# One layer of a hybrid decoder trunk: the last tiles' routing and the first experts' preparation in another order

## The chip, the cores and the metric

The kernel runs on 1 core of a Trainium2 chip. TensorE (PE) multiplies, VectorE (DVE) and ScalarE (ACT) work elementwise, GpSimd (POOL) does some elementwise work and issues the indirect transfers, and SyncE (SP) issues most of the other transfers. All of them run side by side and each takes its instructions strictly in the order in which the program emits them. The metric is device microseconds for one execution, the median of several runs.

## What is computed

One layer of a trunk over 1024 tokens of width 1024. A mixer (a causal convolution branch and an mLSTM branch) ends in `x1 = x + gate1 * (merged W_out)`. Its second half is a mixture of experts, which is what the change is about:

```python
h = modulate(rmsnorm(x1, g_norm2), sh2, sc2)
p_grp = softmax(h @ w_rg + b_rg); g_sel = argmax(p_grp)           # one group of 4
le_sel = (h @ w_re + b_re).reshape(T, 4, 8)[t, g_sel[t]]          # its 8 experts
top_p, top_e = top_k(softmax(le_sel), 2)                          # two of them
w_tok = p_grp[g_sel] * top_p / sum(top_p)
y = sum over the two: w_tok * ((silu(h @ w_e_gate[e]) * (h @ w_e_up[e])) @ w_e_down[e])
out = rmsnorm(x1 + gate2 * y, g_final)
```

There are 32 experts; `w_e_gate`, `w_e_up` and `w_e_down` hold 6 MB of each in float32, together about 201 MB.

## The kernel before

**Order.** The schedule is written out by hand: the order in which the Python code calls the engines is the order on each engine. Float32 products are made in three passes of a split pair (`split`: ACT casts the high part, DVE subtracts it to get the low part), so each operand that is split costs one ACT and one DVE instruction.

**Tiles and routing.** Tokens are cut into 8 tiles `t` of 128. For each tile, `products` multiplies the merged branches by `W_out` in 8 steps `k` (halves `hf` of 512 columns; three matmuls a step and half), `residual` adds `x` on DVE, `second_norm` scales and stores `h2` to `h2_d` in DRAM, `router_T` transposes the tile on PE with a copy on ACT, and `router` makes 36 logits. `choose(a, b)` picks group and experts for tiles a to b-1 on DVE, a chain of some 18 small instructions; `weigh(a, b)` makes the weights in three steps (subtractions and three Exp on ACT; reciprocals and products; a split into bfloat16 columns of `Vc`). Both are generators: `fill` runs one step of what the list `lat` holds, `drain` runs all of it. For t = 4 and 5 they are put into `lat`; for tiles 5, 6 and 7 `choose` is called outright.

**Ranks, keys, selections.** `ranks_early` counts, by matmuls over one-hot rows, how many tokens before each one chose the same expert. `set_key` turns this into a slot number for the experts 0 and 1 (`FIX = 2`), which are handled first without knowing how full the others are. `sel_into(r, sl)` compares an iota with the key to get a selection matrix; `first_slots` multiplies it with the token numbers, `index` turns the sums into indices, and `gather` fetches the expert's rows of `h2_d` by an indirect transfer on POOL into `xgs[r]`, which ACT has cleared before. `order_of_experts` (three steps, `places_`) sorts the experts by their counts, gives the list `elist` from which SP takes the weights' addresses, and gives each token its place `pos` in its expert's block. `st_sel(b)` makes the selection of block `b` (two instructions on DVE, one of them 128x2048), `st_slots(b)` its token indices (16 small matmuls on PE, two instructions on DVE) and the gather, `st_x(b)` the transposed and split input, `st_gu` the gate (`wi = 0`) and up (`wi = 1`) products, `st_act` Silu and the product, `st_h` its transposition, `st_down` the down products and the scatter to `y_d`.

**Weights.** The object `W` streams the experts' weights: each load is 1 MB into one of six buffers `big`; SP issues the next load when a buffer has been split or, for pieces marked plain, has been multiplied. Split parts go to five pairs of buffers. `W.split()` forces the next split; `W.take()` hands out a piece, splits up to `nsplit` pieces ahead and issues loads. Gate of expert 0 has four pieces; the first three are split during tiles 1 to 3.

**Blocks.** `units = [[0], [1], [16], [2, 24], [17], [3], ...]`: in unit i of the loop at the end, the products of unit i+1 are woven with the activation and down products of unit i. Blocks 16 to 23 hold two experts with few tokens, 64 rows each; their pieces are all plain, and their matmuls use half of the array's columns.

Of the kernel before, what the change touches and what calls it, by code (L numbers as in the profile page):

```python
# [8 lines left out]
F32 = mybir.dt.float32  # L9
# [33 lines left out]
def hybrid_layer_kernel(ctx: ExitStack, tc: tile.TileContext, x, c, w_ada, b_ada, g_norm1, w_in, b_if,  # L43
# [11 lines left out]
    def tt(o, a, b, op, eng=V):  # L55
        return eng.tensor_tensor(out=o, in0=a, in1=b, op=op)  # L56

    def ts(o, a, s1, op0, s2=None, op1=None, eng=V):
        if op1 is None:
            return eng.tensor_scalar(out=o, in0=a, scalar1=s1, scalar2=None, op0=op0)  # L60
        return eng.tensor_scalar(out=o, in0=a, scalar1=s1, scalar2=s2, op0=op0, op1=op1)
# [1058 lines left out]
    def k3(ap):  # L1120
        return ap.rearrange("p (k q) -> p k q", q=P)
# [85 lines left out]
    lsg = rp.tile([P, NT, NE], F32, name="lsg")  # L1207
    rev = rp.tile([P, EPG], F32, name="rev")
    t4 = [rp.tile([P, NT, NG], F32, name=f"t4{i}") for i in range(3)]
    t8 = [rp.tile([P, NT, EPG], F32, name=f"t8{i}") for i in range(6)]  # L1210
# [125 lines left out]
    def order_of_experts():  # L1336
# [16 lines left out]
        ts(bs[0:NE], idn, rc, OP.mult)  # L1353
        ts(tw[0:NE], ion[0:NE], rc, OP.is_equal)
        yield 0
        psx = mps.tile([P, 512], F32, tag="m", name="psord")
# [10 lines left out]
        yield 0  # L1367
        kp = mo.tile([P, NT, NE], F32, tag="tHL", bufs=2, name="kp")
        ts(kp, rank, float(P), OP.is_ge, float(P * (TWB - FIX - 1)), OP.mult)
        tt(kp, kp, rank, OP.add)  # L1370
        tt(kp, kp, cb(bs, NE), OP.add)
# [104 lines left out]
    for t in range(NT):  # L1476
# [18 lines left out]
        if t < NT - 1:  # L1495
            for k in range(KT):
                products(k, (0, 1))
                if k == 2 and t > 0:
                    router_T(t - 1)
                if k == 5 and t > 0:  # L1500
                    router(t - 1)
                    if t == NT - 2:
                        for _ in choose(t - 1, t):
                            pass
            if t == 0:
                router_const()
            if t in (4, 5):
                a_, b_ = ((0, 3), (3, 5))[t - 4]
                lat.extend((choose(a_, b_), weigh(a_, b_)))
            for _ in range(6 if t < 6 else 20):  # L1510
                fill(0)
            for hf in range(2):
                residual(t, hf)
            second_norm(t)
        else:
            for k in range(KT):
                products(k, (0,))
                if k == 3:
                    router_T(t - 1)
            router(t - 1)  # L1520
            for _ in choose(t - 1, t):
                pass
            residual(t, 0)
            scale_half(t, 0)
            po[t][1] = zps.tile([P, 2, 512], F32, tag="z", name=f"o{t}_1")[:, 0, :]
            for k in range(KT):
                if k == KT - 1:
                    router(t, (0,))
                products(k, (1,))
                if k == 3:  # L1530
                    router_T(t, (0,))
                if k == 5:
                    ranks_early()
                    set_key(slice(0, LT), psr[0][:, 0:LT])
                    S.copy(rank[:, 0:LT], psr[0][:, 0:LT])
    sel01 = uo.tile([P, FIX, NT, P], BF16, tag="ar", bufs=2, name="sel01")
    psf = {}
# [10 lines left out]

    sel_into(0, slice(0, LT))
    yp.release()  # L1550
# [18 lines left out]
    xgs = [e4(f"xg{i}") for i in range(3)]  # L1569
    for g_ in xgs:  # L1570
        S.activation(k3(g_), iota.unsqueeze(1).broadcast_to([P, KT, P]), AF.Copy, scale=0.0)
    for _ in choose(LT, NT):
        pass
# [46 lines left out]
    def ovf_slots(pool, bv, name):  # L1620
# [12 lines left out]
        return idx, wsl, ps, osel  # L1633

    identb = rp.tile([P, P], BF16, name="identb")
    V.tensor_copy(identb, ident)

# [154 lines left out]
    for r in range(FIX):  # L1792
        if r:
            sel_into(r, slice(0, LT))
        sel_into(r, slice(LT, NT))
        first_slots(r, LT if r == 0 else 0, NT)
        idx = mo.tile([P, 1], I32, tag="fidx", name=f"fidx{r}")
        index(mo, idx, psf[r], 0, f"f{r}")
        gather(xgs[r], idx)
        R[r] = dict(xg=xgs[r])  # L1800
# [5 lines left out]
    rest = weigh(LT - 2, NT)  # L1806
    next(rest)
    next(places_)
    st_x(0)
    W.split()  # L1810
    W.split()
    next(rest)
    next(places_)
    for _ in rest:
        pass
    W.nsplit = 4
    st_gu(0, 0, 0, 4)
    for b in blocks_of(2):
        st_sel(b)
    W.split()  # L1820
    W.split()
    st_x(1)
    st_gu(0, 1, 0, 2)
    for b in blocks_of(2):
        st_slots(b)
    st_sel(0)
    st_gu(0, 1, 2, 4)
    st_slots(0, False)
# [36 lines left out]
    for i, unit in enumerate(units):  # L1865
# [3 lines left out]
        st_act(unit[-1])  # L1869
        for b in blocks_of(i + 3) if i else []:  # L1870
            st_slots(b)
# [9 lines left out]
        for b in now:  # L1881
            st_x(b)
        for b in blocks_of(i + 4) if i else []:
            st_sel(b)
        if i == 0:
            for b in units[3]:
                st_sel(b)
        fill(0)
        fill(0)
        if not nxt:  # L1890
# [180 lines left out]
```

## Time and profile before

| what | value |
|---|---|
| median of 3 runs | 1435.85 us (1435.72 to 1435.99) |
| the profiled execution | 1434.2 us, span 1432.4 us from first to last instruction |
| mean granted TensorE clock | 0.963 of full speed |
| busy: PE, DVE, ACT, POOL | 1303.9, 999.9, 513.7, 326.8 us |
| moved by DMA | 337.13 MB |
| last tile's routing to first expert | about 779 to 812 us of the span |

The times in all views count from the start of the span. In a row of the timeline the columns are start, duration, engine, line, operation, what it writes and reads, partitions and elements, and how many are merged; brackets give the idle time of the engine before it and what ended that. Names are those of the program without numbers: `mg` is the tile `x1`, `o` the products with `W_out`, `sel` any selection, `sl` and `slf` slot sums, `tpx` and `tph` transposes of an expert's input and hidden values, `gu` gate and up products, `py` down products, `wh` and `wl` the split weights. A line is often a helper's (L56 `tt`, L60 and L61 `ts`, L64 `stt`, L67 `mm`, L148 the cast in `split`).

### The profile page before, as it was taken

The numbers are of one execution on the slowest core, as the hardware profiler recorded it, in microseconds if no ns is written. First come the engines' busy times: TensorE is split into PE (matmuls) and PEld (weight loads), VectorE is DVE, ScalarE is ACT, GpSimd is POOL, SyncE is SP. The second block draws the span as 40 slices with busy tenths as digits, with TensorE's granted clock in tenths as the row PEclk, the third lists the DMA queues.
The fourth block names the chain that finished last, engine by engine and source line by source line (L and its number), as shares of the span: only waits on it lengthen the run. The fifth ranks groups of instructions, "written<-read, shape, count | busy, mean of one in ns | idle before, by whom it ended". The sixth has DMA issues, their size and how long they took to land. (4 is left out here: it accounts for less than half of the span.)

```text
span 1432.4 us, 17703 instructions
## 1 busy us (share of the span) xinstructions
PE 1303.9 (91%) x6627; PEld 973.3 (68%) x6627; DVE 999.9 (70%) x1371; ACT 513.7 (36%) x682; POOL 326.8 (23%) x265
## 2 busy tenths in 40 slices
PE   4799989999989999999999679999899999999976
PEld 3687888879878888777887445656465565654554
DVE  6979998889976761655556685457676675754587
ACT  5233143333532224411222323335344353533442
POOL 3333455231331310115222010001111111110033
PEclk9799989999999999999999899999999999999998
DMA  9433443333353433444521578899999999999982
GB/s 288 126 118 133 140 140 119 132 118 88 115 175 125 154 114 129 168 155 154 175 102 59 191 259 331 331 379 407 418 414 404 407 401 402 405 385 399 397 337 119
DMA packets 121161, 337.13 MB, mean 235 GB/s; under 512 B 12481, under 2 KB 74221, under 8 KB 96240
## 3 DMA queue, kind: packets, MB, share of 16 engines
q1 hardware_dynamic: 106064, 290.81, 54.4%
q0 software_dynamic: 14528, 43.56, 8.1%
q10 hardware_dynamic: 480, 1.59, 0.3%
q8 instruction: 53, 0.87, 0.2%
q14 instruction: 36, 0.29, 0.1%
HBM read 303.37 MB, written 41.45 MB: 241 GB/s over the span
## 5 line engine op out<-in xcount | busy, mean ns | idle before, releaser
L56 DVE TENSOR_TENSOR wl<-big,wh 128x1024 fp32r<-128x1024 f32 x184 | 224.7, 1256 | 104.5 <-ACT wh L148 103.4
L148 ACT CAST wh<-big 128x1024 fp32r<-128x1024 f32 x184 | 185.5, 1048 | 174.8 <-DMA big<-in_w_e_gate_dram 90.8
L64 DVE SCALAR_TENSOR_TENSOR cacc<-u,vec,cacc 128x1024 f32<-128x1024 f32 x120 | 212.0, 1767 | 2.9
L67 PE MATMUL z<-hH,wh 128*128 128x512 f32 x512 | 166.3, 407 | 7.4 <-DVE hH L377 5.1
L67 PE MATMUL gu<-wh,tHLx 128*128 128x512 f32 x528 | 169.3, 401 | 2.6 <-ACT wh L148 2.6
L67 PE MATMUL z<-hL,wh 128*128 128x512 f32 x512 | 163.0, 400 | 1.4 <-DVE hL L56 1.2
L67 PE MATMUL z<-hH,wl 128*128 128x512 f32 x512 | 162.2, 398 | 0.0
L67 PE MATMUL gu<-big,tFx 128*64 128x512 f32 (+1 forms) x528 | 131.8, 628 | 0.0
L67 PEld LDWEIGHTS gu<-wh,tHLx 128*128 128x128 f32 x528 | 96.7, 189 | 29.5 <-ACT wh L148 9.5
L67 PEld LDWEIGHTS z<-hH,wh 128*128 128x128 f32 x512 | 96.2, 192 | 29.3 <-ACT hH L380 5.1
L67 PEld LDWEIGHTS z<-hL,wh 128*128 128x128 f32 x512 | 97.3, 190 | 26.1 <-DVE hL L56 1.9
L67 PEld LDWEIGHTS z<-hH,wl 128*128 128x128 f32 x512 | 97.3, 190 | 23.6 <-DVE wl L56 0.2
L67 PE MATMUL gu<-wl,tHLx 128*128 128x512 f32 x264 | 106.1, 402 | 7.7 <-DVE wl L56 7.6
L1617 POOL DMA_INDIRECT y_d<-ye,idx x23 | 32.6, 1416 | 339.1 <-DVE ye L64 319.0
L56 DVE TENSOR_TENSOR wl<-raw,wh 128x1024 fp32r<-128x1024 f32 (+1 forms) x45 | 70.7, 1575 | 39.5 <-ACT wh L148 39.5
L67 PEld LDWEIGHTS gu<-big,tFx 128*64 128x64 f32 (+1 forms) x528 | 39.8, 146 | 73.7 <-issue 71.6
L56 POOL TENSOR_TENSOR acc<-acc,ar 128x1024 f32<-128x1024 f32 x24 | 70.5, 2939 | 61.5 <-ACT ar L572 51.8
L67 PE MATMUL zt<-wl,hH 128*128 128x256 f32 (+1 forms) x256 | 76.1, 297 | 4.5 <-DVE wl L56 4.5
L67 PE MATMUL zt<-wh,hH 128*128 128x256 f32 (+1 forms) x256 | 77.3, 302 | 0.8 <-ACT qk L659 0.7
L67 PE MATMUL zt<-wh,hL 128*128 128x256 f32 (+1 forms) x256 | 76.2, 298 | 0.0
L67 PE MATMUL o<-woH,mHL 128*128 128x512 f32 x256 | 72.9, 401 | 0.0
L67 PE MATMUL py<-wh,tHLh 128*128 128x512 f32 x256 | 72.5, 405 | 0.1
(403 smaller groups left out, 2193.2 us busy)
## 6 DMA issues: line engine op xcount, KB each, us to landing
big<-in_w_e_gate_dram SPq DMA_DIRECT2D x64, 1024.0 KB
big<-in_w_e_up_dram SPq DMA_DIRECT2D x64, 1024.0 KB
big<-in_w_e_down_dram SPq DMA_DIRECT2D x64, 1024.0 KB
raw<-in_w_in_dram SPq DMA_DIRECT2D x38, 512.0 KB
ar<-in_w_ada_dram SPq DMA_DIRECT2D x16, 1024.0 KB
araw<-in_w_ada_dram SPq DMA_DIRECT2D x8, 1024.0 KB
y_d<-zero SPq DMA_DIRECT2D x16, 512.0 KB
big<-y_d SPq DMA_DIRECT2D x9, 512.0 KB
```

The costliest lines, as they stand in the source:

```text
L56: return eng.tensor_tensor(out=o, in0=a, in1=b, op=op)
L64: return V.scalar_tensor_tensor(out=o, in0=a, scalar=s, in1=b, op0=op0, op1=op1)
L67: return PE.matmul(o, l, r, start=start, stop=stop)
L148: S.copy(h, src)
L1617: G.indirect_dma_start(out=y_d[:, :], out_offset=bass.IndirectOffsetOnAxis(ap=idx[:, 1:2], axis=0), in_=src, in_offset=None, bounds_check= ...
```

## The change

It reorders what is emitted; nothing is computed differently. Part by part: (1) `identb`, a bfloat16 identity, is made at the set-up. (2) In tile 6, `drain` runs what is left of `weigh(3, 5)` at step k = 1 instead of after the products. (3) In tile 7, `router_T(6)` and `router(6)` come earlier among the first half's products, and in the second half `router_T(7)`, the ranks and the first half of `router(7)` come later. (4) Both selections of tiles 0 to 6 for the experts 0 and 1 are made together before `residual(7, 1)`. (5) The third buffer for gathered rows is cleared later. (6) In `order_of_experts` the first two instructions on `kp` move from the third step to the first. (7) After the three Exp of tiles 5 to 7, ACT runs a Silu on one column. (8) Gate piece 3 of expert 0 is split right behind that, gate pieces 0 to 2 of expert 1 only after the gate products of expert 0 (before: pieces 0 ahead of them, 1 and 2 behind). (9) The selection of block 16 comes before, that of block 0 in front of the up products of expert 0, and both sets of slots behind all of them. (10) In unit 1 of the loop, `st_slots(17)` comes after the gate products of block 16, the transposes of unit 1 and `st_x(2)`. (11) The two `fill(0)` of every unit are gone; the one thing left in `lat`, the check for overflowing experts (`overflow`), runs in unit 4 instead of unit 0.

```diff
+    identb = rp.tile([P, P], BF16, name="identb")
+    V.tensor_copy(identb, ident)
...
+        kp = mo.tile([P, NT, NE], F32, tag="tHL", bufs=2, name="kp")
+        ts(kp, rank, float(P), OP.is_ge, float(P * (TWB - FIX - 1)), OP.mult)
+        tt(kp, kp, rank, OP.add)
         yield 0
...
-        kp = mo.tile([P, NT, NE], F32, tag="tHL", bufs=2, name="kp")
-        ts(kp, rank, float(P), OP.is_ge, float(P * (TWB - FIX - 1)), OP.mult)
-        tt(kp, kp, rank, OP.add)
...
                 products(k, (0, 1))
+                if k == 1 and t == NT - 2:
+                    drain()
...
-            for _ in range(6 if t < 6 else 20):
+            for _ in range(6):
                 fill(0)
...
                 products(k, (0,))
-                if k == 3:
+                if k == 2:
                     router_T(t - 1)
-            router(t - 1)
+                if k == 5:
+                    router(t - 1)
...
             for k in range(KT):
-                if k == KT - 1:
-                    router(t, (0,))
                 products(k, (1,))
-                if k == 3:
+                if k == 4:
                     router_T(t, (0,))
-                if k == 5:
+                if k == 6:
                     ranks_early()
...
+            router(t, (0,))
...
-    sel_into(0, slice(0, LT))
+    for r in range(FIX):
+        sel_into(r, slice(0, LT))
...
-    for g_ in xgs:
+    def clear_xg(g_):
         S.activation(k3(g_), iota.unsqueeze(1).broadcast_to([P, KT, P]), AF.Copy, scale=0.0)
+    for g_ in xgs[0:2]:
+        clear_xg(g_)
...
     for r in range(FIX):
-        if r:
-            sel_into(r, slice(0, LT))
         sel_into(r, slice(LT, NT))
...
     next(places_)
     rest = weigh(LT - 2, NT)
     next(rest)
+    S.activation(mo.tile([P, 1], F32, tag="silu", bufs=1, name="silu"), pio, AF.Silu)
+    W.split()
+    clear_xg(xgs[2])
     next(places_)
     st_x(0)
-    W.split()
-    W.split()
+    next(places_)
     next(rest)
-    next(places_)
     for _ in rest:
         pass
     W.nsplit = 4
-    st_gu(0, 0, 0, 4)
     for b in blocks_of(2):
         st_sel(b)
+    st_gu(0, 0, 0, 4)
+    W.split()
     W.split()
     W.split()
     st_x(1)
-    st_gu(0, 1, 0, 2)
+    st_sel(0)
+    st_gu(0, 1, 0, 4)
     for b in blocks_of(2):
         st_slots(b)
-    st_sel(0)
-    st_gu(0, 1, 2, 4)
     st_slots(0, False)
...
-        for b in blocks_of(i + 3) if i else []:
+        for b in blocks_of(i + 3) if i > 1 else []:
             st_slots(b)
...
         for b in now:
             st_x(b)
+        for b in blocks_of(i + 3) if i == 1 else []:
+            st_slots(b)
...
-        fill(0)
-        fill(0)
+        if i == 4:
+            drain()
```

## Rows read from the trace of the kernel before

**Rows 1.** Windows: length, busy time of PE, PEld, DVE, ACT, POOL; granted clock, DMA share, GB/s.

```profile
803.00:868.00 65.00, 50.44 (x276) 30.95 (x277) 45.94 (x113) 18.64 (x28) 9.97 (x7) 0.84 0.53 187
900.00:960.00 60.00, 59.91 (x310) 35.95 (x308) 29.51 (x35) 18.31 (x24) 6.32 (x5) 1.00 0.88 345
960.00:1350.00 390.00, 364.54 (x1839) 219.04 (x1836) 248.60 (x280) 169.38 (x203) 43.88 (x33) 0.99 1.00 404
860.50:866.20 5.70, 5.70 (x17) 1.43 (x14) 0.00 (x0) 0.00 (x0) 1.00 (x1) 0.60 0.37 111
```

**Rows 2.** Timeline of PE, first experts.

```profile
827.62 0.59 PE L67 MATMUL sl<-Vc,sel 128*128 128x9 bf16 x16 [4.23 <-DVE sel L56]
...
833.76 0.56 PE L67 MATMUL sl<-Vc,sel 128*128 128x9 bf16 x16 [0.58 <-DVE sel L56]
...
841.74 1.13 PE L1673 MATMUL tpx<-ident,xg 128*128 128x128 f32 x8 [1.29 <-DMA xg<-h_d,idx]
...
859.45 0.59 PE L67 MATMUL sl<-Vc,sel 128*128 128x9 bf16 x16 [2.87 <-DVE sel L56]
859.98 6.18 PE L67 MATMUL gu<-big,tFx 128*64 128x512 f32 x16
...
866.77 3.65 PE L67 MATMUL gu<-big,tFx 128*64 128x512 f32 x16
```

**Rows 3.** Timeline of SP: the first two up loads of block 16.

```profile
866.19 0.94 SPq L204 DMA_DIRECT2D big<-in_w_e_up_dram  x2
```

**Rows 4.** Timeline of DVE, tiles 6 and 7.

```profile
776.57 0.19 DVE L56 TENSOR_TENSOR oab<-oh,oh 128x32 bf16<-128x32 f32 x1
...
779.11 1.29 DVE L56 TENSOR_TENSOR mg<-o,xr 128x512 f32<-128x512 f32 x2
...
793.43 1.09 DVE L56 TENSOR_TENSOR sel<-iota,key 128x896 bf16<-128x896 f32 x1
795.56 0.69 DVE L56 TENSOR_TENSOR mg<-o,xr 128x512 f32<-128x512 f32 x1 [1.04 <-PE o L67]
```

**Rows 5.** Timeline of PE, tile 7: the last product step of a half, then a router.

```profile
783.11 0.63 PE L67 MATMUL o<-woH,mHL 128*128 128x512 f32 x2
...
783.81 1.87 PE L67 MATMUL psl<-wrs,x1T 128*128 128x36 f32 x16
```

**Rows 6.** Timeline of ACT: the third Exp of tiles 5 to 7, and the first Silu's table.

```profile
809.20 0.19 ACT L1294 ACTIVATE t<-t 128x3 f32<-128x3 f32 x1
...
833.26 1.28 ACT L1743 ACT_TABLE_LOAD   x1 [12.60 <-PE gu L67]
```

**Rows 7.** The page's costliest groups: splits of the experts' weights (busy, mean ns).

```profile
L56 DVE TENSOR_TENSOR wl<-big,wh 128x1024 fp32r<-128x1024 f32 x184 | 224.7, 1256 | 104.5 <-ACT wh L148 103.4
L148 ACT CAST wh<-big 128x1024 fp32r<-128x1024 f32 x184 | 185.5, 1048 | 174.8 <-DMA big<-in_w_e_gate_dram 90.8
```

**Rows 8.** Timeline of ACT, an earlier change of tables.

```profile
359.87 1.28 ACT L768 ACT_TABLE_LOAD   x1
361.20 1.28 ACT L768 ACTIVATE WT<-WT,ga 128x128 f32<-128x128 f32 x4
```

**Rows 9.** Timeline of DVE, first expert's input to the selection of block 0.

```profile
812.37 0.69 DVE L56 TENSOR_TENSOR tHLx<-tpx,tHLx 128x512 fp32r<-128x512 f32 x1 [1.18 <-ACT tHLx L148]
...
816.49 2.36 DVE L56 TENSOR_TENSOR wl<-big,wh 128x1024 fp32r<-128x1024 f32 x2 [1.60 <-ACT wh L148]
...
831.41 2.29 DVE L56 TENSOR_TENSOR sel<-iota,pm 128x2048 bf16<-128x2048 f32 x1
```

**Rows 10.** Timeline of POOL: the gather of block 16.

```profile
832.05 2.52 POOL L1612 DMA_INDIRECT xg<-h_d,idx  x1 [23.25 <-issue]
```

**Rows 11.** The gathers' line from 800 to 960 us: durations (ns min/median/max), landing.

```profile
L1612 POOL DMA_INDIRECT xg<-h_d,idx x7: 998/1284/2521, 832.1 to 949.6; - x7
...
DMA to landing us min/median/max: 4.3/8.0/10.9
```

**Rows 12.** Timeline of DVE in unit 4.

```profile
962.28 3.72 DVE L56 TENSOR_TENSOR wl<-big,wh 128x1024 fp32r<-128x1024 f32 x3 [3.75 <-ACT wh L148]
```

More of the change, by code (lines that the diff above doesn't have):

```diff
@@ L1633, in ovf_slots @@
         return idx, wsl, ps, osel
-    identb = rp.tile([P, P], BF16, name="identb")
-    V.tensor_copy(identb, ident)
     def by_slot(o, sel):
```

## Prediction

> **What bounds the kernel now.** I read the windows first, because a share of busy time says nothing across stages. In [rows 1] three stages stand apart. From 960 to 1350 us the DMA share is 1.00 and PE is busy for 364.5 of 390 us: the experts' weights set the pace, and no order of instructions makes them fewer. From 900 to 960 PE is busy for 59.9 of 60 us at a DMA share of 0.88: PE sets the pace. From 803 to 868 neither does: PE stands for 14.6 of 65 us, its granted clock averages 0.84 of full speed, and at a share of 0.53 DMA idles for 30.5 us. Loads can't run ahead there, since the six buffers are full until PE or DVE frees one. So a microsecond won before 868 is won by PE and by the weights together, and both carry it to the end.
>
> Second came PE's waits in that stage. [Rows 2] name them: 4.23 us for the selection of block 16, 0.58 for that of block 0, 1.29 for block 16's gathered rows, 2.87 for the selection of block 17. After the last one PE runs at half speed: 16 half-array matmuls take 6.18 us at 859.98 and 3.65 at 866.77; the window from 860.5 to 866.2 [rows 1] has a granted clock of 0.60 (it averages the levels 1.2 and 2.4 GHz). Third came SP's queue: the next two loads, the up weights of block 16, are issued at 866.19 [rows 3], just as those 16 matmuls end (859.98 + 6.18). DMA had run dry, with a share of 0.37 in that window. I take this issue as the marker: before it stand the edits' effects, after it PE and DMA are both full, and the rest should move as a block.
>
> **Tiles 6 and 7.** In tile 6 the remaining steps of `weigh(3, 5)` fill DVE between the end of `choose` (776.57 + 0.19) and the residual at 779.11 [rows 4]: 2.35 us go from there. They move to where DVE waits for `router(5)`, and cost nothing; without that cover they would delay those logits by the same 2.35. Then `router_T(6)` and `router(6)` have three product steps between them instead of four; one step is 783.81 - 783.11 = 0.70 us [rows 5]. So tile 6's logits, choices and `residual(7, 0)` come 3.05 us earlier. PE, no longer waiting for them, starts the second half at about 783.8, has eight steps of 0.70 and an estimated 1 us of transposes and ranks in it, and is done at about 790.4. What is late next is DVE: keys at 789.7 and then two selections of 1.09 us [rows 4], one of them new in this place, to 792.3. The second residual, which waited for PE at 795.56, comes 3.3 us earlier and now waits for DVE.
>
> From there the chain runs as before: logits, choice, rank, key, first gathers, counts, order. Behind it the selection for expert 1 (1.09) and `identb` are gone, of which I keep 0.8, since the counts then wait for PE's small matmuls; the two `kp` instructions (an estimated 0.75) come in front. The third Exp, which ended at 809.4 [rows 6], ends at about 806.1: 3.3 us earlier.
>
> **ACT's new order.** Behind the Exp ACT now has the table load (1.28, [rows 6]) with its one-column Silu (0.2), the cast of gate piece 3 (1.05, [rows 7]) and the clear of the third buffer, a same-sized pass (1.05), and only then the cast of expert 0's input: at 809.7. DVE meanwhile waits for the cast, subtracts (1.25, [rows 7]) to 809.9, and does the second step of `order_of_experts` (about 1.1) behind it, which delays `elist` and the capacities. The input's first subtraction comes at 811.0 instead of 812.37 [rows 9]. So 1.4 of the 3.3 us are left here. The early table saves nothing by itself: in its old place ACT had been idle for 12.6 us and PE had other matmuls to do.
>
> An earlier change of tables shows what stands around the load: nothing ahead of it, and the next activation 1.33 us after its start [rows 8]. The Trainium skill, "ScalarE: Activation LUTs", section "What ACT_TABLE_LOAD costs", counts 1283 ns of load and about 1380 ns of drain for a change of table. The load agrees with 1.28 us here, the drain is not seen; by that page ACT's chain would be 1.4 us longer, and my estimate of the whole gain 8.4 us instead of the sum below.
>
> **DVE to the selection of block 0.** Before, the second input subtraction ended at 814.9 (816.49 less the wait of 1.60, [rows 9]); two splits ended at 818.85, small instructions filled 6.4 us, and the selection of block 16 (2.29) ended just ahead of PE's 827.62. After: subtraction over at 813.5, no splits in between, 5.7 us of small instructions (`kp` is gone), selection over at 821.5. That is 6 us earlier, while PE is still at expert 0's products, and the 4.23 us wait goes. Then three splits (3.6), two input subtractions of expert 1 (1.25) and the selection of block 0 (2.45) end at 828.8. PE gets there at about 826.5 (it reached 823.4 before, half of the up products are still to be added, about 4 us, less some 1) and stands for 2 us: the wait that takes the old one's place. The slots of block 0 move from 833.76 to 828.8: 5.0 us.
>
> **The gather of block 16.** Its index now waits behind that selection and one more split on DVE: issue at about 829.9 instead of 832.05 [rows 10], 2.1 us earlier. PE, which needs 840.45 - 833.76 = 6.7 us from the slots to the transposes [rows 2], would be there at 835.5. The rows landed at 841.7, 9.65 us after issue. Landing took 4.3 to 10.9 us among the gathers [rows 11]; I take 7.0, the nearer to the middle, because the loads beside it start some 5 us earlier (the split that frees their buffer does) and are nearly through. Transposes at 836.9: 4.85 us earlier.
>
> In the old order the gather's own 2.52 us [rows 10] ran beside the 2.29 us selection at 831.41 [rows 9], while the shortest took 1.0 [rows 11]. The Trainium skill, "SBUF — State Buffer", section "SBUF: two separate sides", says that VectorE and GpSimd lock a shared port pair against each other, so that descriptors wait for a DVE instruction. The rows fit it. By that rule the gather would now stand beside a 1.25 us split, land about 1.2 us sooner, and the estimated gain would be 11.0.
>
> **Block 17 and the clock.** From those transposes to the place of the 2.87 us wait PE has 856.6 - 841.7 = 14.8 us of work, unchanged. Without the wait and with the 0.56 us of `sl` moved behind, block 16's gate products start at 851.7 instead of 859.98: 8.3 us. If the clock doesn't fall there, they take 3.65 instead of 6.18 [rows 2], and end at 855.4 instead of 866.16. DMA, moved by 4.85, has work until about 856.4 (it had 0.37 x 5.7 = 2.1 us of it after 860.5). So the loads of [rows 3] follow without a gap, **9.8 us** earlier. PE, with `sl` (0.56) given back and a wait of 0.5 (0 to 1.3) because the slot sums now take another of four PSUM buffers, which expert 1's down product needs next, is 9.7 us earlier: the two agree.
>
> **Edits at nothing.** `overflow` (some 2.3 us of DVE) goes to unit 4, where DVE idles for 3.75 us ahead of the splits at 962.28 [rows 12]; without that cover it would delay the splits and so the loads by up to 2.3. Block 17's gather is issued behind `st_x(2)` but is needed a unit later. The dropped `fill` calls had nothing else to run. SP's order of loads is the same; only their waits end earlier.
>
> **The sum.** The profiled execution took 1434.2 us, 1.65 below the median of the runs. 1434.2 - 9.8 = 1424.4; on the scale of the median 1435.85 - 9.8 = **1426.0 us**. Ends: the gather (4.3: 1.4 better, up to PE's own arrival; 10.9: 3.9 worse), the clock at block 16 (2.5 worse), the PSUM wait (0.8 worse, 0.5 better), a fall of the clock after the new 2 us wait (up to 2.5 worse, as in [rows 2], partly hidden by the gather). The likeliest case lies between 1423.5 and 1429.
>
> **Rivals.** (a) *The gather stays slow and the clock stays low*: 9.8 - 2.65 (9.65 us landing) - 2.5 = 4.7 us, 1431. For it: the gather meets the same kind of loads. Against: it starts with fewer of them queued. (b) *The weights set the end whatever PE does*: 1435.9. For it 390 us at a share of 1.00; against it the 30.5 us in which DMA idles just before. (c) *ACT's new order starves the gather, slower*: if tile 7 gives back nothing, DVE still has 3.7 us more ahead of the index (a split, a selection), the gather lands at about 845.4, PE stands for 5 us, and the clock then costs 2.5 as in [rows 2]. With block 17's 3.4 us taken off and the low clock staying at block 16, that is 3 us more: 1439. It decides once the landing is later than about 845. (d) *The gaps of DMA from 900 to 960 close as well*, since PE gets further ahead of the weights: up to 7.2 us more, 1419. Against it: PE is full there.
>
> **How the numbers follow.** A difference under 0.2% (2.9 us) can't be told from none. Forecast 0.58, (a) 0.23, (b) 0.09, (c) 0.07, (d) 0.03. Forecast, (a) and (d) are faster: 0.84; (b) same: 0.09; (c) slower: 0.07. The range 1423 to 1432.5 holds the forecast and nearly all of (a), and leaves out (b), (c) and (d).
>
> **What would show it.** Right: the second residual of tile 7 near 792; Silu's table right behind the Exp; no wait of PE for block 16's selection, one of about 2 us for block 0's; transposes of block 16 near 837; block 16's first gate products in about 3.7 us; the loads of [rows 3] near 856 with no hole in DMA. Wrong: a landing near 840, half speed at block 16, or the 9.8 us shrinking between 868 and 960, which would mean that PE and the weights don't move as one block.

## The result and the profile after

The changed kernel took 1425.12 us in the median (1422.26 to 1429.44, 4 runs), the kernel before 1435.92 (1435.72 to 1436.04, 4 runs): a ratio of 0.9927, 95% interval 0.9902 to 0.9953. It is 10.8 us faster; 9.8 were forecast. The runs of the changed kernel scatter by 7 us, and the profiled one is the slowest of them: 1429.44 us with a span of 1427.7, 4.7 less than the span before. So the profile has to be read for where time was won, and more runs have to say how much.

First the windows of the changed kernel (columns as in [rows 1]):

```profile
803.00:856.00 53.00, 43.76 (x230) 29.10 (x232) 38.93 (x81) 17.61 (x26) 7.50 (x6) 0.87 0.54 201
...
950.00:1350.00 400.00, 374.93 (x1878) 225.60 (x1874) 257.74 (x301) 172.07 (x205) 44.25 (x34) 0.98 1.00 402
...
836.00:840.00 4.00, 1.46 (x10) 1.25 (x11) 0.00 (x0) 0.69 (x2) 0.00 (x0) 1.00 0.14 56
840.00:844.00 4.00, 4.00 (x11) 1.83 (x10) 2.64 (x3) 4.00 (x5) 0.00 (x0) 1.00 0.00 0
...
844.00:857.00 13.00, 13.00 (x95) 7.72 (x94) 9.65 (x15) 0.76 (x2) 4.26 (x3) 1.00 0.97 367
...
857.00:950.80 93.80, 90.25 (x468) 56.18 (x470) 46.88 (x58) 29.80 (x39) 11.13 (x8) 0.98 0.88 349
```

The stage in which neither PE nor DMA was full ends at 856 instead of 868. PE stands for 9.2 us of it (14.6 before) and DMA for 24.4, that is 53 x (1 - 0.54), where it was 30.5. DMA is still nearly empty from 836 to 844, while PE waits for the rows of block 16 and then works through expert 0's down product. From 844 it is full, with no hole at block 16's gate products.

Second, PE's timeline of the changed kernel:

```profile
826.88 0.55 PE L67 MATMUL sl<-Vc,sel 128*128 128x9 bf16 x16
828.28 0.56 PE L67 MATMUL sl<-Vc,sel 128*128 128x9 bf16 x16 [0.85 <-DVE sel L56]
...
838.54 1.12 PE L1679 MATMUL tpx<-ident,xg 128*128 128x128 f32 x8 [3.58 <-DMA xg<-h_d,idx]
...
853.29 3.65 PE L67 MATMUL gu<-big,tFx 128*64 128x512 f32 x16
...
863.38 0.97 PE L67 MATMUL py<-wh,tHLh 128*128 128x512 f32 x3 [0.36 <-DVE tHLx L56]
...
883.49 0.75 PE L1679 MATMUL tph<-ident,hs 128*128 128x128 f32 x4 [3.10 <-DVE hs L56]
...
894.07 1.51 PE L67 MATMUL py<-big,tFh 128*64 128x512 f32 x6
```

Against [rows 2]: the wait of 4.23 us for block 16's selection is gone, that for block 0's grew from 0.58 to 0.85, that for the gathered rows from 1.29 to 3.58, and the 2.87 for block 17's selection is gone. Block 16's first 16 gate products took 3.65 us instead of 6.18. The loads that [rows 3] show at 866.19 are issued at 856.97, on SP's timeline:

```profile
856.97 5.56 SPq L204 DMA_DIRECT2D big<-in_w_e_up_dram  x4
```

This marker, 9.2 us earlier, is the forecast's 9.8. Behind it the lead shrinks: counted by the same load in both traces, it is 9.2 us at the 16th load after the first, 7.6 at the 24th, 5.4 at the 40th, 3.7 at the last, and 4.7 at the end of the span. That shrinking is what the prediction said would make its last step wrong. (At the first of these loads, 687.14 before and 686.33 here, 0.8 us of the lead stand already. That is scatter of the start: in another execution of the changed kernel, e1_again, the same load comes at 688.78.)

### The profile page after: what moved, and what is told of

It is laid out like the page before. It is cut to its first block, busy times and chain, and to the rows that moved or that the text cites. A ratio compares the mean times of both kernels' runs of the same rounds, so it can differ in the third digit from the quotient of the medians.

```text
span 1427.7 us, 17703 instructions
## 1 busy us (share of the span) xinstructions
PE 1304.7 (91%) x6627; PEld 975.6 (68%) x6627; DVE 999.0 (70%) x1371; ACT 514.0 (36%) x683; POOL 327.0 (23%) x265
```

## The experiments

The kernels were timed in three groups, each on one chip and beside the kernel before. The medians of the kernel before were 1435.97, 1436.43 and 1435.59 us in the three groups. All kernels compute everything. "Marker" is the issue of block 16's first up loads, counted from the issue of the first expert weights (these shift by up to 3.6 us from run to run, so times of two profiles are compared below as counted from this issue, where the text says so); "cast" is the start of the first split of block 2's gate weights behind the marker; both are from the one profiled execution of each.

| kernel | median us (range, runs) | ratio (95% interval) | marker | cast |
|---|---|---|---|---|
| before (its profile) | 1435.92 (1435.72–1436.04, 4) | | 179.0 | 16.7 |
| after (its profile) | 1425.12 (1422.26–1429.44, 4) | 0.9927 (0.9902–0.9953) | 170.6 | 18.4 |
| e1_again: after, unchanged | 1429.65 (1425.51–1431.56, 7) | 0.9947 (0.9928–0.9966) | 169.8 | 18.0 |
| e2_17_old_place | 1431.14 (1424.8–1433.85, 10) | 0.9961 (0.9942–0.998) | 175.7 | 15.5 |
| e5_16_between | 1427.44 (1424.13–1428.43, 6) | 0.9933 (0.9913–0.9954) | 169.8 | 18.7 |
| e6_17_in_unit2 | 1425.34 (1420.55–1428.44, 6) | 0.9922 (0.9898–0.9946) | 170.8 | 17.1 |
| e3_tiles_only | 1432.72 (1426.43–1435.14, 12) | 0.9973 (0.9959–0.9986) | 175.8 | 16.6 |
| e8_experts_only | 1431.46 (1426.25–1435.94, 12) | 0.9963 (0.9948–0.9978) | 171.1 | 17.9 |
| e4_no_early_silu | 1428.04 (1421.5–1432.23, 6) | 0.9932 (0.9908–0.9956) | 170.8 | 18.8 |
| e7_all_three | 1424.64 (1422.79–1426.67, 6) | 0.9912 (0.9896–0.9928) | 168.0 | 17.2 |
| e9_before_again: before, unchanged | 1435.31 (1432.85–1438.85, 12) | 1.0002 (0.9987–1.0018) | 179.4 | 16.5 |
| e10_16_and_17 | 1427.05 (1426.54–1429.82, 6) | 0.9951 (0.9934–0.9969) | 169.6 | 16.9 |
| e11_16_at_once | 1423.43 (1419.01–1427.71, 6) | 0.9917 (0.9895–0.9939) | 167.2 | 16.8 |
| e12_again2: after, unchanged | 1426.98 (1422.55–1434.21, 12) | 0.9944 (0.9926–0.9961) | 168.2 | 19.3 |

### How far a run can be trusted: e1_again, e9_before_again, e12_again2

No edit: the changed kernel twice more, the kernel before once.

> The changed kernel unchanged, to see which part of its profile repeats. Block theory (what is won before 868 us reaches the end whole): the two up loads of block 16 are issued near 857, the gate loads of blocks 3 and 17 and all behind them stand about 9 us earlier than before, median near 1425. Weights theory (from 857 on the transfers set the pace, and block 17's gather, now in the full stretch, costs them 1.2 us and PE more): the same issue near 857, but PE's wait ahead of the transposes of block 16's hidden values is 2 to 3 us, and the lead at 960 us is between 5 and 8 us, differing from run to run with the clock behind that wait.

> The changed kernel once more, for the pool of its runs and a third profile: issue of block 16's up loads 169.8 to 170.6 us after the first weight load, first cast of block 2's gate 18.0 to 18.4 us behind it, median 1425 to 1430.

> The kernel before, timed against itself: a second profile, and what the measurement makes of no change at all. Both theories: the same waits, the issue of block 16's up loads 179 us after the first weight load, 37 us from there to the second group of gate loads. If the weights' stage behind 960 us differs from run to run by itself (394 to 397 us between the same two loads in kernels that are alike there), it shows here too: ratio within 0.998 to 1.002 and a stage length other than 394.0.

The change is worth 10.8, 6.3 (1435.97 - 1429.65) and 8.6 us (1435.59 - 1426.98) in three series; all 23 timed runs of it have a median of 1427.03 us. The kernel before against itself comes out at 1.0002, yet its own runs in these groups reach from 1429.2 to 1441.8. The spread has a place in the traces: from the 50th load after the first to the last, the same 141 MB in kernels that are alike there, 394.0 to 397.3 us passed among the profiled executions (394.0 and 395.3 in the kernel before alone). So a single execution can't show 2 us at its end. Nor can the marker as it stands, which is 170.6, 169.8 and 168.2 in three profiles of the changed kernel. But what differs there is one transfer: PE took block 16's rows 9.30, 8.24 and 6.69 us after the issue of their gather (this is called the landing below), and with it taken off 161.3, 161.6 and 161.5 are left. e12's marker and its cast (19.3) lie outside what the first two profiles had led to expect; the landing accounts for the marker. The experiments below are read at the marker first, with the landing beside it.

### The two halves: e3_tiles_only, e8_experts_only

e3 keeps parts 1 to 4 and 6 of the change and has all else as before; e8 is the converse. Of e3's edit to the changed kernel, the core:

```diff
-    S.activation(mo.tile([P, 1], F32, tag="silu", bufs=1, name="silu"), pio, AF.Silu)
-    W.split()
-    clear_xg(xgs[2])
...
+    st_gu(0, 0, 0, 4)
     for b in blocks_of(2):
         st_sel(b)
-    st_gu(0, 0, 0, 4)
...
-    st_sel(0)
-    st_gu(0, 1, 0, 4)
+    st_gu(0, 1, 0, 2)
     for b in blocks_of(2):
         st_slots(b)
+    st_sel(0)
+    st_gu(0, 1, 2, 4)
```

> Only the edits to tiles 6 and 7, the first selections, the bfloat16 identity and the two early instructions of the third step; the experts' part as before. Block theory: the logits' chain is 3.3 us earlier, the first gathers 2.4 to 3.3 us, and all that hangs behind them: 1432.5, 3.3 us faster than before. Rival (the wait only moves): the first experts' part is bound by DVE's splits and selections of its own, and less than 1.5 us are left: 1434.5 or more.

> Only the edits to the experts' part (early Silu, splits, selections and slots of blocks 16, 0 and 17, the third buffer's clear, the overflow check); tiles 6 and 7 and the first selections as before. Block theory: the up loads of block 16 come 9.2 - 3.3 = about 6 us earlier: 1430. Weights theory: the wait and clock behind 857 take 2 us of it: 1432. Rival (ACT's new order alone makes the gather of block 16 later): slower than 1434.

The tiles alone gave 3.7 us (1436.43 - 1432.72), with the marker 3.2 earlier; the working had 3.3. PE then stood 2.55 us for block 16's selection, 2.05 for block 0's and 2.86 for block 17's, and the 16 gate products behind that took 6.22 us. The experts alone gave 5.0 us, with the marker 7.9 earlier. Timelines of POOL and of PE in e8:

```profile
833.72 0.99 POOL L1616 DMA_INDIRECT xg<-h_d,idx  x1 [24.63 <-issue]
```

```profile
832.75 0.56 PE L67 MATMUL sl<-Vc,sel 128*128 128x9 bf16 x16 [2.60 <-DVE sel L56]
...
840.11 1.14 PE L1677 MATMUL tpx<-ident,xg 128*128 128x128 f32 x8 [0.68 <-DMA xg<-h_d,idx]
```

Without the gain in the tiles the gather is issued 1.7 us later than in the kernel before (1.4 counted from the first weights), just as rival (c) feared. But PE takes its rows 6.4 us after that, at 840.1, before the point (845) from which that rival would have decided. At the marker 3.2 + 7.9 = 11.1 against 8.4 (after), 9.2 (e1) and 10.8 (e12) for the whole. The landing differs too: 9.69 us before, 8.94 in e3, 6.39 in e8. With it taken off, the marker stands at 169.4 before (168.6 in e9), 166.9 in e3, 164.8 in e8 and 161.3 to 161.6 in the changed kernel: of the whole 7.8 to 8.0, the tiles hold 2.5 and the experts 4.6. The parts add to within 1 us, about as well as the two profiles of the kernel before agree.

### Block 17's slots: e2_17_old_place, e6_17_in_unit2

e2 takes part 10 back; e6 goes further and puts block 17's slots and gather into unit 2, at the same place among the unit's steps.

```diff
 # e2
-        for b in blocks_of(i + 3) if i > 1 else []:
+        for b in blocks_of(i + 3) if i else []:
             st_slots(b)
...
-        for b in blocks_of(i + 3) if i == 1 else []:
-            st_slots(b)
 # e6
-        for b in blocks_of(i + 3) if i == 1 else []:
+        for b in units[4] if i == 2 else []:
             st_slots(b)
```

> The changed kernel with the slots and the gather of block 17 back in their old place, right behind the activation of unit 1. Block theory: the wait for the selection comes back (2.9 us) and half clock behind it (2.5 us): median 5.4 us above the changed kernel, near 1430. Weights theory: the wait comes back, but the gather lands ahead of the full stretch and 1 to 3 us of it are regained by 890: 2 to 4 us above the changed kernel, near 1428.

> The changed kernel with the slots and the gather of block 17 moved on to unit 2, behind the gate products of blocks 2 and 24, where the DMA share was 0.3 (892 to 900 us). Block theory: nothing changes, PE has the same work: 1425 within 1 us. Weights theory: the second gate load of block 2 lands 1.2 us earlier, PE's wait ahead of the transposes of block 16's hidden values falls from 3.1 to about 1.8 us and its clock stays up behind it: 1.5 to 3 us faster than the changed kernel, near 1423.

PE in e2, its timeline:

```profile
855.94 0.56 PE L67 MATMUL sl<-Vc,sel 128*128 128x9 bf16 x16 [2.86 <-DVE sel L56]
856.43 5.35 PE L67 MATMUL gu<-big,tFx 128*64 128x512 f32 x16
...
884.75 0.75 PE L1679 MATMUL tph<-ident,hs 128*128 128x128 f32 x4 [0.30 <-DVE hs L56]
```

The wait for block 17's selection is back with 2.86 us, and behind it the clock falls (a granted clock of 0.68 from 856.4 to 861.8; 5.35 us for what takes 3.65). The marker is 5.9 us later than in e1. But the medians differ by 1.5 us only (1431.14 and 1429.65, and the intervals overlap), and the last line says where a part of the rest went: PE's wait for block 16's activations, 2.44 us in e1, is 0.30 here. In e2 the first cast of block 2's gate starts 15.5 us behind the marker, in e1 18.0.

Why, is seen at POOL. First the kernel before, then the changed one, then e6:

```profile
861.20 1.00 POOL L1612 DMA_INDIRECT xg<-h_d,idx  x1 [5.51 <-issue]
```

```profile
829.25 0.99 POOL L1621 DMA_INDIRECT xg<-h_d,idx  x1 [22.90 <-ACT wh L148]
...
864.94 2.53 POOL L1621 DMA_INDIRECT xg<-h_d,idx  x1 [12.46 <-PE py L67]
```

```profile
892.66 3.00 POOL L1621 DMA_INDIRECT xg<-h_d,idx  x1 [7.92 <-DVE pm L60]
```

Block 17's gather ran at 861.20, in the hole that DMA had there (share 0.37 in [rows 1]). In the changed kernel it is issued 8 us behind the marker, in a stretch in which DMA is full. Its 128 rows of 4 KB are 0.52 MB, at the 349 GB/s of that stretch 1.5 us. The kernels fall into groups by the place of this gather: the cast comes 15.5 to 16.7 us behind the marker with it in the hole (before, e2, e3, e9), 17.9 to 19.3 with it in the full stretch (after, e1, e4, e5, e8, e12), 16.8 to 17.2 with it in unit 2 (e6, e7, e10, e11). The groups' means are 16.3, 18.5 and 17.0, and they don't overlap. The hole's group differs in more than the gather, though: in the 3 us before its marker DMA's share is 0.38 to 0.55, in all others 0.97 to 1.01, so its loads found fewer ahead of them. The cleaner comparison is that with unit 2, where the gather's place and the 0.56 us of block 17's slots beside it are the whole edit: 1.5 us, which is what its size and the rate give. By medians e6 is 4.3 us better than e1 on the same chip, but the intervals overlap, and e10, which has the same move and e5's, is no better than e12: the cost is shown in the traces, not in the times. Neither theory of the expectations got the sizes: e2 stayed below the 5.4 us of the one and the 2 to 4 of the other, and in e6 PE still waits 2.25 us for block 16's activations where 1.8 had been expected.

### The gather of block 16 and Silu's table: e5_16_between, e4_no_early_silu

e5 issues block 16's gather before the selection of block 0; e4 leaves the early Silu out.

```diff
 # e5
-    st_sel(0)
-    st_gu(0, 1, 0, 4)
+    st_gu(0, 1, 0, 2)
     for b in blocks_of(2):
         st_slots(b)
+    st_sel(0)
+    st_gu(0, 1, 2, 4)
 # e4
-    S.activation(mo.tile([P, 1], F32, tag="silu", bufs=1, name="silu"), pio, AF.Silu)
```

> The changed kernel with the slots and the gather of block 16 between the two halves of expert 0's up products, ahead of the selection of block 0 on DVE. The gather starts about 2.4 us earlier (near 826.8), and PE's wait for its rows falls from 3.6 to about 1.2 us. Block theory: all of it reaches the end: 2.4 us faster than the changed kernel, near 1422.7. Weights theory: the transfers have nothing to do from 837 to 843 in the changed kernel because no buffer is free, so this too starts them earlier and gives 2.4 us; only what comes behind 857 is given back: 1.2 to 2.4 us.

> The changed kernel without the one-column Silu behind the Exp, so that its table is loaded at expert 0's activation again. If the early load stands in the way (my reading): ACT's cast of gate piece 3 and DVE behind it come 1.4 us earlier, the gather of block 16 too, and PE, which waits 3.6 us for its rows, gains up to 1.4: 1423.7. If the early load is what takes a wait off the activation: the hidden values of expert 0 come 1.3 us later and PE waits for them: 1425 or 1426. The skill's page on activation tables (2.66 us for a change) would make the gain of leaving it out 2.7.

In e5 the gather is issued 2.45 us earlier than in e1 (same chip), counted from the first weights; but its issue takes 2.52 us again, since it stands beside the 2.29 us selection, and the landing takes 10.65 us instead of 8.24. PE takes the rows at the same time in both, 151.4 us behind the first weights, and the marker is the same 169.8. Issued earlier, landing slower: nothing gained. In e4 the gather is issued 1.0 us earlier than in e1, counted likewise, where 1.4 had been expected, and PE then waits no less for its rows. Behind that wait the clock falls. PE in e4, its timeline:

```profile
839.13 1.94 PE L1679 MATMUL tpx<-ident,xg 128*128 128x128 f32 x8 [2.96 <-DMA xg<-h_d,idx]
840.87 7.80 PE L67 MATMUL py<-big,tFh 128*128 128x512 f32 x16
```

The granted clock is 0.58 from 839 to 843, and the two rows take 1.94 and 7.80 us where the changed kernel's take 1.12 and 7.03; in that kernel PE had waited longer (3.58 us) and the clock stayed up. So e4's marker comes 1.6 us later than its landing alone would put it. Its ratio, 0.9932, can't be told from e1's 0.9947. The table load itself stands at 827.19 there, and PE waits for nothing that hangs on it: in that the prediction was right, the early table saves nothing by itself. What it costs e4 can't show, with the clock fallen.

### Together: e7_all_three, e10_16_and_17, e11_16_at_once

e7 has the edits of e4, e5 and e6, e10 those of e5 and e6. e11 has e4's and e6's, and issues block 16's gather as soon as its selection is done:

```diff
+    st_x(1)
+    st_gu(0, 1, 0, 1)
+    for b in blocks_of(2):
+        st_slots(b)
     W.split()
     W.split()
     W.split()
-    st_x(1)
     st_sel(0)
-    st_gu(0, 1, 0, 4)
-    for b in blocks_of(2):
-        st_slots(b)
-    st_slots(0, False)
+    st_gu(0, 1, 1, 4)
...
+        if i == 0:
+            st_slots(0, False)
```

> The changed kernel with three edits: block 16's slots between the halves of expert 0's up products, block 17's in unit 2, no early Silu. If each expectation holds by itself (2.4, 1.5 to 3 and up to 1.4 us) and they add up: 1418.5 to 1421. If the wait for block 16's rows (3.6 us) is the shared limit of the first and the third: 1420 to 1422.

> The changed kernel with block 16's slots between the halves of expert 0's up products and block 17's in unit 2, early Silu kept. Against the kernel with all three edits this tells what the early table is worth. If it stands in the way: gather of block 16 about 0.9 us later than there and the time 1 us higher, 1425.5; if it is free: the same 1424.6. The first cast of block 2's gate comes 17.1 us behind the issue of block 16's up loads (17.9 to 18.8 with block 17's gather in that stretch).

> No early Silu, block 17's slots in unit 2, block 16's slots behind the first quarter of expert 0's up products and ahead of the three splits, block 0's slots behind the transposes of block 16. Block 16's gather starts about 4 us earlier than with all three edits, PE waits for nothing up to its transposes (2.7 us at block 0's slots gone), which come near 834. Block theory: 1.8 to 2.5 us faster than with all three edits, 1422.5. Weights theory: up to the issue of block 16's up loads the same, then more is given back: 1423.5 to 1424.6.

The parts did not add up in e7: 1418.5 to 1422 us had been expected and 1424.64 came out. Behind PE's wait for block 16's activations (2.26 us) the clock fell there, which had not been counted. Between e7 and e10 the early table is the only difference. With it (e10) the gather is issued 0.95 us later, counted from the first weights, and the marker stands 1.6 us later (169.6 and 168.0). The ratios are 0.9951 and 0.9912, with intervals that just don't overlap (0.9934 to 0.9969, 0.9896 to 0.9928). So beside the other two edits the early table does seem to cost; but the two were timed on different chips, and the size is open.

POOL and PE in e11, two timelines:

```profile
824.49 1.26 POOL L1621 DMA_INDIRECT xg<-h_d,idx  x1 [16.47 <-issue]
```

```profile
834.26 1.06 PE L1679 MATMUL tpx<-ident,xg 128*128 128x128 f32 x8
...
849.79 0.50 PE L67 MATMUL gu<-wl,tHLx 128*128 128x512 f32 x1 [1.60 <-DVE wl L56]
...
878.88 0.75 PE L1679 MATMUL tph<-ident,hs 128*128 128x128 f32 x4 [1.24 <-DVE hs L56]
```

PE no longer waits for the rows, and the marker is the earliest of all (167.2). A new wait of 1.60 us, for expert 1's splits, takes part of it. With 1423.43 us, 12.2 below the kernel before on its chip, e11 has the lowest median of the study and e7 the lowest ratio; e11's interval overlaps with that of the changed kernel in e12 beside it (0.9926 to 0.9961), and e7 and e11 can't be told apart. They are the versions to go on with, not shown winners.

## Why the prediction was right, step by step

**Tiles 6 and 7: right in kind, a quarter too large.** The timeline of DVE in the changed kernel, which answers to [rows 4, 9]:

```profile
790.33 2.09 DVE L56 TENSOR_TENSOR sel<-iota,key 128x896 bf16<-128x896 f32 x2
792.34 0.69 DVE L56 TENSOR_TENSOR mg<-o,xr 128x512 f32<-128x512 f32 x1
...
810.67 0.68 DVE L56 TENSOR_TENSOR tHLx<-tpx,tHLx 128x512 fp32r<-128x512 f32 x1
...
818.92 2.29 DVE L56 TENSOR_TENSOR sel<-iota,pm 128x2048 bf16<-128x2048 f32 x1
...
825.93 2.29 DVE L56 TENSOR_TENSOR sel<-iota,pm 128x2048 bf16<-128x2048 f32 x1
...
880.41 1.23 DVE L56 TENSOR_TENSOR wl<-big,wh 128x1024 fp32r<-128x1024 f32 x1 [1.65 <-ACT wh L148]
881.56 1.28 DVE L56 TENSOR_TENSOR tHLx<-tpx,tHLx 128x512 fp32r<-128x512 f32 x2
882.76 0.68 DVE L56 TENSOR_TENSOR hs<-gu,hs 128x512 f32<-128x512 f32 x1
```

The second residual of tile 7 starts at 792.34 (792.3 forecast) and now waits for DVE's two selections; the first subtraction of expert 0's input comes at 810.67 (811.0); the selection of block 16 is over at 821.21 (821.5), that of block 0 at 828.22 (828.8). That these agree to some tenths is in part luck, since this profile's first weights come 0.8 us earlier than those of the kernel before. Counted from the first weights, the three profiles of the changed kernel have the residual 2.1 to 2.4 us earlier than the kernel before (3.3 forecast), the end of the third Exp 2.3 to 2.6 (3.3), the subtraction 0.7 to 0.9 (1.4), the end of block 16's selection 5.3 to 5.5 (6) and that of block 0's 4.4 to 4.7 (5). The term was 2.5 us rather than 3.3, and e3 shows the same by itself: 3.7 us in the medians and 3.2 at the marker, of which 0.75 are a shorter landing.

**ACT's order: right.** Its timeline, which answers to [rows 6, 8]:

```profile
805.82 0.19 ACT L1296 ACTIVATE t<-t 128x3 f32<-128x3 f32 x1
806.01 1.28 ACT L1812 ACT_TABLE_LOAD   x1
807.31 0.20 ACT L1812 ACTIVATE silu<-pio 128x1 f32<-128x1 f32 x1
807.42 1.03 ACT L148 CAST wh<-big 128x1024 fp32r<-128x1024 f32 x1
808.35 1.05 ACT L1577 ACTIVATE xg<-iota 128x1024 f32<-128x1024 f32 x1
809.39 0.58 ACT L148 CAST tHLx<-tpx 128x512 fp32r<-128x512 f32 x1
...
875.33 1.99 ACT L148 CAST wh<-big 128x1024 fp32r<-128x1024 f32 x2 [11.42 <-DMA big<-in_w_e_gate_dram]
...
879.33 1.05 ACT L148 CAST wh<-big 128x1024 fp32r<-128x1024 f32 x1 [2.01 <-DMA big<-in_w_e_gate_dram]
```

The third Exp ends at 806.01 (806.1), the cast comes at 809.39 (809.7). Between the table load and the next activation 1.30 us pass, all of it the load. The drain of about 1380 ns that the Trainium skill, "ScalarE: Activation LUTs", section "What ACT_TABLE_LOAD costs", adds to it does not stand there, so ACT's chain did not grow by the 1.4 us that the page's figure would have meant.

**The gather: the mis-sized term.** It was issued at 829.25 (829.9), but PE took the rows at 838.54: 9.3 us instead of 7.0, inside the bounds kept (4.3 to 10.9), and the transposes were 3.2 us earlier instead of 4.85. In the three profiles of the changed kernel the landing took 9.3, 8.2 and 6.7 us. PE's new wait in front of block 0's slots, forecast at 2 us, was 0.85. Behind the rows all came as worked out: gate products at 853.29 (851.7) at full clock, a PSUM wait of 0.36 us (0.5), the marker at 856.97 (856.4), set by the end of those products (856.94). The working's 856.4 does not follow from its own terms: DMA's work, which by the rows lasted until 860.5 + 2.1 = 862.6, ends at 857.7 when it moves by 4.85, and the products were to end at 855.4.

The issue itself took 0.99 us instead of 2.52, as the rule in the Trainium skill, "SBUF — State Buffer", section "SBUF: two separate sides", had it (an instruction of VectorE with two inputs in SBUF locks out a GpSimd operation that reads SBUF), and the runs follow that rule further: seven gathers of block 16 issued in 0.99 us (after, e1, e2, e4, e6, e8, e12) landed after 6.4 to 9.3 us, mean 8.2; five issued in 2.52 beside a selection (before, e9, e3, e5, e10) after 8.9 to 10.8, mean 10.1 (1.5 of the difference is the issue itself). In e7, also issued in 2.52, PE came later than the rows, which the trace has landed after 8.3. Block 17's gather went the other way, from 1.00 to 2.53 us.

**The step that failed: "Block 17's gather is issued behind `st_x(2)` but is needed a unit later", costed at nothing.** PE indeed didn't wait for it. But it was cheap before because it lay in a hole of DMA, and the change closes that hole. Behind the marker the loads pay for it: the casts come 1.5 us later in the mean with the gather in the full stretch than with it in unit 2 (18.5 and 17.0 in e2's section), and 2.2 later than with it in the hole, where the emptier queue counts as well. What then waits is shown by the last lines of the two fences above: the cast at 879.33 waits for the loads of block 2's gate, the split at 880.41 for that cast, and `hs` of block 16 stands behind both on DVE at 882.76. PE, which needs `hs`, stands 3.10 us at 883.49; before it was 1.75:

```profile
890.58 0.75 PE L1673 MATMUL tph<-ident,hs 128*128 128x128 f32 x4 [1.75 <-DVE hs L56]
```

So PE and the weights didn't "move as a block". The loss has two parts. From the marker to the 28th load after the first the lead falls from 7.6 to 6.1 us in e1, whose clock stays up: 1.5 us, by which `hs` comes later behind the marker. It falls by 3.7 in the changed kernel's first profile and by 3.9 in e12: 2.1 and 2.4 us of it by the later `hs`, and 1.5 more because the clock fell behind that wait (from there to the 28th load 14.3 and 14.2 us passed, 12.7 in e1 and in the kernel before). The prediction had allowed for a fall of the clock at block 16's products and behind the wait for block 0's slots, not here. In the 93.8 us behind the marker DMA's share is 0.88 in the changed kernel's first profile; the windows of the kernel before and of e1:

```profile
866.20:960.00 93.80, 91.84 (x470) 55.83 (x472) 48.95 (x57) 29.80 (x39) 8.61 (x7) 1.00 0.91 359
```

```profile
858.60:952.40 93.80, 90.91 (x478) 55.84 (x480) 49.07 (x59) 29.80 (x39) 11.14 (x8) 1.00 0.91 360
```

That is 11.3 us of idle DMA in the changed kernel against 8.4 in both others: DMA idles longer only where the clock fell. In e1 it is as busy as before, and the loss of 1.5 us is the size of the gather that it now also moves there. Most of the rest of what is missing at the end of the first profile is 1.6 us in the stage of the weights (395.6 us instead of 394.0), which lies inside its spread between executions alike.

**The rivals.** (a) was half right: the gather stayed slow (9.3 us) in one profile of three, the clock at block 16 in none. (b), that the weights set the end, is true of a part: of the lead at the marker 4.5 us are gone at the end of the span in the changed kernel's profile, 4.5 in e1 and 5.3 in e12, against the profile of before; and e2, 5.9 us behind e1 at the marker, is 1.5 behind it in the median. (c) is refuted by e8. (d) didn't come. `overflow` in unit 4 was free: its instructions fill DVE up to 955.5, and DVE then still waits 1.46 us for the same splits that it waited 3.75 for in [rows 12]:

```profile
953.34 1.77 DVE L64 SCALAR_TENSOR_TENSOR nbs<-nbd,nbs 128x32 f32<-128x32 f32 x8
...
956.96 3.70 DVE L56 TENSOR_TENSOR wl<-big,wh 128x1024 fp32r<-128x1024 f32 x3 [1.46 <-ACT wh L148]
```

**What stays open.** The forecast of 1426.0 agrees with 1427.03 over all runs, with 8.4 to 10.8 us at the marker (counted from the first weights) where 9.8 were forecast, and a loss behind it of which nothing was forecast. So the close agreement of the time is in part luck: the spans of the three profiled executions are 3.1 to 4.7 us shorter than that of the kernel before, the medians 6.3 to 10.8. How many us that loss is worth in the median was not settled: the scatter of the stage of the weights is larger.

## What to carry to other kernels

A wait that is removed ahead of a saturated stage also closes the hole in which other transfers ran for nothing: list what lay in the hole, and price each piece of it at the rate of the full stretch. Where two engines are full behind the edit, take the gain at a marker (here the first load that the edit frees) and then follow it load by load to the end, since the instructions queued behind a late load can hand a part back. And time a kernel against itself first: a change of 2 us can be read in a trace here once the landing of one gather is taken off, and can't in a median.

## What the runs showed of the hardware

**The clock fell behind one wait and not behind its like.** At 884 us the granted clock of the changed kernel averages 0.58, between its levels of 1.2 and 2.4 GHz, and the matmuls that stand there take 1.06 us where their like take 0.62 or 0.63. Windows of the changed kernel, then of e1, the same kernel:

```profile
880.00:884.00 4.00, 0.90 (x7) 0.51 (x5) 3.55 (x7) 2.79 (x5) 0.00 (x0) 1.00 1.00 385
884.00:888.00 4.00, 4.00 (x13) 3.17 (x13) 3.21 (x3) 0.59 (x1) 1.28 (x1) 0.58 0.99 408
```

```profile
881.00:885.00 4.00, 1.56 (x10) 1.04 (x8) 3.57 (x7) 2.77 (x5) 0.00 (x0) 1.00 1.00 395
885.00:889.00 4.00, 4.00 (x20) 3.26 (x20) 3.19 (x3) 0.59 (x1) 1.28 (x1) 1.00 1.01 426
```

The waits were 3.10 and 2.44 us. It fell as well in e12 (wait of 2.61 us, granted clock 0.61 over 4 us), e10 (2.55 and 0.60) and e7 (2.26 and 0.70), and stayed at 1.00 in e5 (2.64), e6 (2.25), e4 (2.20) and e8 (2.02). In front of block 16's rows it fell in e4 (2.96) and not in the changed kernel (3.58). What decides between them was not found; a stall of 2 to 3.6 us ahead of products cost another 1.5 us here or nothing.

**A gather's issue ends 0.9 us behind the VectorE instruction beside it.** In the kernel before, block 16's gather is issued at 832.05 beside the selection that ends at 833.70 (831.41 + 2.29), and the issue ends 0.87 us later, at 834.57. It is the same throughout: over the 14 profiles 199 gathers start while a block's selection (128x2048) or the split of a piece of weights (128x1024) runs on VectorE, and the issue of each ends 0.86 to 0.92 us after that instruction, nearly the 1.0 us that an issue with nothing beside it takes. In e6, to the row at 892.66 above, this is:

```profile
892.50 2.29 DVE L56 TENSOR_TENSOR sel<-iota,pm 128x2048 bf16<-128x2048 f32 x1
```

The selection ends at 894.79, the issue at 895.66. In the changed kernel block 16's gather starts 0.1 us behind the product `hs`, which reads PSUM, and takes its 0.99 us all the same.

**A gather's landing is not set by its issue alone.** For the same 128 rows it took 6.4 to 10.8 us over the profiles. In the three profiles of the changed kernel the issues, counted from the first weights, are within 0.3 us of each other (142.9 to 143.2) and gave 6.7 to 9.3. The loads in flight beside it have a part in it. By the trace's own landing times e11's gather landed 4.7 us after its issue, the quickest of block 16's, and no packet moved from 824 to 826 us there; block 17's landed after 4.2 or 4.3 us in the hole (before, e3, e9) and after 10.8 to 11.2 in the full stretch (e5, e8, e12), of which 1.5 are the longer issue. What makes the 6.4 to 9.3 among gathers issued alike was not separated.
